# Wider up-projection matmuls, one-pass biased scores, summed head groups and later side work in a two-layer encoder kernel

## The chip, the cores and the metric

The kernel runs on 1 core of one Trainium2 chip. The metric is device time in microseconds (us): the median of 3 runs was 2298.27 us (2297.31 to 2302.01). Engines are named as in the profile: PE (TensorE matmuls), PEld (its weight loads), DVE (VectorE), ACT (ScalarE), POOL (GpSimd), SP (SyncE, whose queue issues the DMAs).

## What is computed

Two encoder layers on x of 256 tokens by 2048 features, all in fp32. The reference, cut to what matters:

```python
for layer in range(2):
    sh1, sc1, g1, sh2, sc2, g2 = split(silu(c) @ ada_w[layer] + ada_b[layer], 6)
    h = rms_norm(x, norm_g[layer, 0]) * (1 + sc1) + sh1
    y = local_dilated_mixer(h, ...) if layer == 0 else diff_attention(h, ...)
    x = x + g1 * rms_norm(y, norm_g[layer, 1])
    h = rms_norm(x, norm_g[layer, 2]) * (1 + sc2) + sh2
    gate, up = split(h @ w_up, 2)                       # 2 x 5504 columns
    gate = gate[t-1] * w[0] + gate[t] * w[1] + gate[t+1] * w[2] + b
    x = x + g2 * rms_norm((gelu(gate) * up) @ w_down, norm_g[layer, 3])
```

Layer 0's mixer has four heads A (one score map, window 128, a sink logit) and four heads B, each with three groups of queries over the same keys and values: the groups' softmax outputs are merged by their denominators, which is one softmax over the three score maps side by side. Layer 1's mixer has eight heads with two score maps each, whose softmaxes are subtracted (weight lambda). Every score has a bias of minus slope times distance.

## The kernel before

**The stream.** Every weight is read once, as tiles `raw` of 128x1024 fp32 (512 KB) in a ring of 9 buffers, in one fixed sequence of "units" (projection weights) and modulation tiles (`ada_w`). ACT rounds a unit to `whi` (fp32r, L248), DVE takes the rest `wlo = raw - whi` (L298); there are four buffers of this pair. A product of activation and weight is three matmuls: high by high, high by low, low by high. A modulation tile is not split: DVE multiplies it with a column of silu(c) and adds it to `aacc` (L273); after 16 tiles `ada_finish` sums over the partitions on PE (L433 and L441).

**Two forms of projection.** `tok_units` (L600 to L602) holds 128 tokens of activation as the stationary operand and streams 512 weight columns. `feat_units` (L629, L631, L632) holds 128x128 of a weight and streams 256 tokens, so a result has features on its partitions: per 128 rows of the contraction and 128 output features, `whi` by `hT` high, `whi` by `hT` low, `wlo` by `hT` high, three matmuls of 256 columns into the same half of a PSUM bank (`packed` holds two such halves). The FFN's gate and up projections and the queries and keys of both layers use it; the high and low parts of `hT` lie side by side, 2x256 columns.

**Order.** `st.done` after each unit is a tick: it starts the splits of the next units, runs the work that is due (`st.at`, `st.chain`, one stage of a chain per tick) and then emits the low parts. In layer 0's FFN and in the tails of the output stages the engines PE, DVE and ACT keep the program's order; elsewhere a scheduler places instructions. Layer 0's queries and keys are made in two halves of the contraction (`first_half` on ACT, `second_half` on DVE adds), then the heads run as chains among the units (`attn_a`, `attn_b`; in layer 1 `attn_c`).

**Around the change.** In `attn_b` DVE adds the bias to each of three maps (L737), takes the maximum over all (L740), ACT exponentiates with a sum (L745); two diagonal matrices with the reciprocal denominators (L477) normalise while PE transposes by matmul (`probs_T`, L672: three accumulating matmuls per 128x128 block). `attn_a` does the same with one map (L697, L698). In `attn_c` the bias and maximum are L780 and L782, the transposes L803. The convolution's weights come as rows (`crow`) that PE turns into columns (L387) 7 ticks after their load was issued.

## Time and profile before

| | before |
|---|---|
| median of 3 runs | 2298.27 us |
| the profiled execution: its own time | 2298.01 us |
| its span, first to last instruction | 2296.2 us |
| granted TensorE clock, mean share | 0.977 |
| PE busy | 2209.7 us (96%), 14953 matmul records |
| DVE busy | 1628.5 us (71%) |
| ACT busy | 1064.3 us (46%) |
| DMA | 588.18 MB, mean 256 GB/s |
| chain that ended last | PE 85%, issue 9%, DVE 2%, ACT 1%, DMA 1% |

In time order: modulation and layer 0's projections to about 190 us, its heads and output projection to 346, a tail of norms to 382, layer 0's FFN to 1120, layer 1's values from 1136, its heads from 1230 to 1475, its output projection to 1545, its FFN to 2278. A fp32 matmul (neither operand fp32r) leaves two records, so the 64 transposing matmuls of L672 are 128 records. The busy time of PE counts the modelled ends of pipelined matmuls; the pitch from start to start is what a matmul costs.

### The profile page before, as it was taken

To read this page: it belongs to the slowest core of one execution; us is meant where nothing else is said; L and a number is where in the kernel's file an instruction comes from. 1 tells how busy PE (TensorE), PEld (TensorE's weight loads), DVE (VectorE), ACT (ScalarE), POOL (GpSimd) and SP (SyncE) were. 2 spreads that over 40 slices of the span, in tenths; PEclk is the share of its full clock that TensorE was granted. 3 is DMA by queue.
4 is the path that set the end of the run, shared out by engine and by line. 5 is a ranking of instruction groups with operands and counts; after the bars stand their busy time and mean duration, and the time that the engine had idled before them with its cause. 6 is when DMAs were issued, how large, how long until landed. Compare 5 with 4: busy or idle time off the path is not lost.

```text
span 2296.2 us, 37376 instructions
## 1 busy us (share of the span) xinstructions
PE 2209.7 (96%) x14953; PEld 2029.4 (88%) x14953; DVE 1628.5 (71%) x1799; ACT 1064.3 (46%) x1463; POOL 42.4 (2%) x72
## 2 busy tenths in 40 slices
PE   4889989999999999999999999999999999999998
PEld 3888876999988999998779998879999888999986
DVE  7779997788776777876788996656656545565555
ACT  4433437454444444444644554456444444444443
POOL 0000000000000000000000100000000000000000
PEclk7989989999999999999999999999999999999999
DMA  9999998988889888997599996655667666667563
GB/s 363 343 329 321 303 340 274 308 287 289 286 287 303 290 285 288 294 294 252 170 337 329 305 306 206 217 179 176 206 198 203 200 203 207 196 202 203 178 186 104
DMA packets 390564, 588.18 MB, mean 256 GB/s; under 512 B 18123, under 2 KB 256373, under 8 KB 389621
## 3 DMA queue, kind: packets, MB, share of 16 engines
q1 hardware_dynamic: 390388, 585.79, 78.4%
q8 instruction: 117, 1.92, 0.4%
q14 instruction: 59, 0.48, 0.1%
HBM read 583.62 MB, written 2.10 MB: 255 GB/s over the span
## 4 chain that ended last, share of the span: by engine, by line
PE 85%; issue 9%; DVE 2%; ACT 1%; DMA 1%; POOL 0%; DVEq 0%; POOLq 0%; SPq 0%; ACTq 0%
PE bank L631 17%; PE bank L629 17%; PE bank L632 17%; PE bank L600 10%; PE bank L601 10%; PE bank L602 10%; DVE aacc L273 1%; PE bank L441 1%; PE bank L775 1%; ACT junk L473 1%; PE bank L812 0%; ACT whi L248 0%; DVE wlo L298 0%; PE bank L433 0%; PE bank L505 0%
## 5 line engine op out<-in xcount | busy, mean ns | idle before, releaser
L298 DVE TENSOR_TENSOR wlo<-raw,whi 128x1024 fp32r<-128x1024 f32 x708 | 860.7, 1219 | 492.6 <-ACT whi L248 473.7
L248 ACT ACTIVATE whi<-raw 128x1024 fp32r<-128x1024 f32 x708 | 745.5, 1055 | 963.6 <-PE bank L631 495.7
L629 PE MATMUL bank<-hT,whi 128*128 128x256 f32 x3616 | 1028.4, 285 | 0.0
L631 PE MATMUL bank<-hT,whi 128*128 128x256 f32 x3616 | 1020.1, 282 | 1.4 <-DVE hT L500 1.4
L632 PE MATMUL bank<-hT,wlo 128*128 128x256 f32 x3616 | 1019.6, 282 | 0.8 <-DVE wlo L298 0.8
L631 PEld LDWEIGHTS bank<-hT,whi 128*128 128x128 f32 x3616 | 687.4, 190 | 4.4 <-DVE hT L500 2.1
L629 PEld LDWEIGHTS bank<-hT,whi 128*128 128x128 f32 x3616 | 687.5, 190 | 2.7 <-ACT whi L248 1.0
L632 PEld LDWEIGHTS bank<-hT,wlo 128*128 128x128 f32 x3616 | 687.1, 190 | 1.4 <-DVE wlo L298 1.2
L273 DVE SCALAR_TENSOR_TENSOR aacc<-raw,ccol,aacc 128x1024 f32<-128x1024 f32 x352 | 455.2, 1293 | 49.8 <-DMA raw<-in_ada_w_dram 48.7
L600 PE MATMUL bank<-whi,act 128*128 128x512 f32 x656 | 259.3, 395 | 0.0
L601 PE MATMUL bank<-wlo,act 128*128 128x512 f32 x656 | 258.9, 395 | 0.0
L602 PE MATMUL bank<-whi,act 128*128 128x512 f32 x656 | 258.9, 395 | 0.0
L602 PEld LDWEIGHTS bank<-whi,act 128*128 128x128 f32 x656 | 123.4, 188 | 29.2
L600 PEld LDWEIGHTS bank<-whi,act 128*128 128x128 f32 x656 | 123.4, 188 | 29.0
L601 PEld LDWEIGHTS bank<-wlo,act 128*128 128x128 f32 x656 | 123.5, 188 | 28.9
L600 PE MATMUL bank<-whi,hT 128*128 128x512 f32 (+1 forms) x192 | 74.9, 393 | 8.5 <-ACT hT L496 8.5
L601 PE MATMUL bank<-wlo,hT 128*128 128x512 f32 (+1 forms) x192 | 74.6, 390 | 0.0
L600 PE MATMUL bank<-whi,oT 128*128 128x512 f32 x176 | 72.8, 414 | 1.0 <-DVE smb L737 1.0
L602 PE MATMUL bank<-whi,hT 128*128 128x512 f32 (+1 forms) x192 | 71.9, 384 | 0.0
L601 PE MATMUL bank<-wlo,oT 128*128 128x512 f32 x176 | 71.0, 404 | 0.0
L602 PE MATMUL bank<-whi,oT 128*128 128x512 f32 x176 | 70.6, 403 | 0.0
L441 PEld LDWEIGHTS bank<-ones,aacc 128*128 128x128 f32 x256 | 37.4, 227 | 25.2 <-issue 22.7
(171 smaller groups left out, 1363.8 us busy)
## 6 DMA issues: line engine op xcount, KB each, us to landing
raw<-in_ada_w_dram SPq DMA_DIRECT2D x384, 512.0 KB, 5.4
raw<-in_ffn_w_up_dram SPq DMA_DIRECT2D x344, 512.0 KB, 4.4
raw<-in_ffn_w_down_dram SPq DMA_DIRECT2D x168, 512.0 KB, 4.8
raw<-in_c_w_in_dram SPq DMA_DIRECT2D x96, 512.0 KB, 5.3
raw<-in_ab_w_in_dram SPq DMA_DIRECT2D x56, 512.0 KB, 5.9
raw<-in_c_w_out_dram SPq DMA_DIRECT2D x32, 512.0 KB, 5.2
raw<-in_ab_w_out_dram SPq DMA_DIRECT2D x16, 512.0 KB, 5.8
gb<-in_norm_g_dram SPq DMA_DIRECT2D x4, 1024.0 KB, 8.0
```

The costliest lines, as they stand in the source:

```text
L248: nc.scalar.activation(hi, v, AF.Copy)
L273: nc.vector.scalar_tensor_tensor(self.acc, t, col, self.acc, op0=ALU.mult, op1=ALU.add)
L298: nc.vector.tensor_tensor(lo, v, hi.bitcast(F32), op=ALU.subtract)
L441: nc.tensor.matmul(t[:, j:j + 1], acc[:, j * P:(j + 1) * P], ones[:, 0:1], start=True, stop=rows is None)
L473: nc.scalar.activation(j[:, :src.shape[1]], src, AF.Square, scale=n ** -0.5, accum_out=dst)
L600: nc.tensor.matmul(dst, ah, hi, start=first, stop=False, skip_group_check=True)
L601: nc.tensor.matmul(dst, ah, lo, start=False, stop=False, skip_group_check=True)
L602: nc.tensor.matmul(dst, al, hi, start=False, stop=last, skip_group_check=True)
L629: nc.tensor.matmul(acc[:, j], wh, hT[:, k, 0], start=k == begin and j == 0, stop=False, skip_group_check=True)
L631: nc.tensor.matmul(acc[:, j], wh, hT[:, k, 1], start=False, stop=False, skip_group_check=True)
L632: nc.tensor.matmul(acc[:, j], wl, hT[:, k, 0], start=False, stop=k == end - 1, skip_group_check=True)
L775: nc.tensor.matmul(s[t][:, j], q[:, j, t * P:(t + 1) * P], k[:, j], start=True, stop=True)
```

## The change

1. `feat_wide` takes the place of `feat_units` in the FFN's up-projections and in layer 1's queries and keys, except for the first seven blocks of layer 0's FFN and the first of layer 1's. `whi` meets high and low of `hT` in one matmul of 512 columns that fills a whole bank, `wlo` meets the high part with 256 columns added to its first half. A block of 256 features so takes two banks, and `both` puts the halves together: ACT copies the second half, DVE adds the first. In the FFN the sum lands in a new tile `gsum`, one tick after the block, from which convolution, taps and product read.
2. `biased` forms the biased scores and their maximum in one instruction (`tensor_tensor_reduce`); the query scale is divided by minus the slope so that (distance + score) times minus the slope is the biased score. It shows as an `ISA` row and a second one of 128x1 that reads the maximum out.
3. `attn_b` adds the three exponentiated maps of a head on DVE, ACT scales by the reciprocal, and `probs_T` is four plain transposes per head; `attn_a` scales likewise. The diagonals are gone.
4. The chain of `attn_c` starts one tick later; the convolution's rows are turned 11 ticks after their load instead of 7; `ada_finish` of the first gates (modulation 2) comes after 6 ticks instead of 2.

```diff
-                    self.at(2, lambda: ada_finish(l, ms, c0, w, acc, rows))
+                    self.at(6 if ms == (2,) else 2, lambda: ada_finish(l, ms, c0, w, acc, rows))
...
+    def feat_wide(n):
+
+        hT = cur["hT"]
+        accs = [packed() for _ in range(n // P)]
+        kt = 0
+        while kt < KT:
+            i, (hi, lo) = st.take()
+            a = hi.shape[1]
+            for b in range(a):
+                k = kt + b
+                for j, acc in enumerate(accs):
+                    nc.tensor.matmul(acc, hi[:, b, j * P:(j + 1) * P], hT[:, k], start=k == 0, stop=False,
+                                     skip_group_check=True)
+                    nc.tensor.matmul(acc[:, 0], lo[:, b, j * P:(j + 1) * P], hT[:, k, 0], start=False,
+                                     stop=k == KT - 1, skip_group_check=True)
+            kt += a
+            st.done(i)
+        return accs
...
+    def biased(dst, dist, s, slope, top):
+        nc.vector.tensor_tensor_reduce(dst, dist, s, -slope, LOWEST, ALU.add, ALU.max, top)
...
-        nc.scalar.activation(dst, acc, AF.Copy, scale=scale)
-
-    def second_half(dst, part, acc, scale=1.0):
-        nc.vector.scalar_tensor_tensor(dst, acc, scale, part, op0=ALU.mult, op1=ALU.add)
+        for d, a, m in scaled_by(scale, dst, acc):
+            nc.scalar.activation(d, a, AF.Copy, scale=m)
+    def second_half(dst, acc, scale=1.0):
+        for d, a, m in scaled_by(scale, dst, acc):
+            nc.vector.scalar_tensor_tensor(d, a, m, d, op0=ALU.mult, op1=ALU.add)
+    def scaled_by(scale, dst, acc):
+        if isinstance(scale, tuple):
+            return [(dst[:, i], acc[:, i], m) for i, m in enumerate(scale)]
+        return [(dst, acc, scale)]
+    def q_scale(*slopes):
+        return tuple(-QK_SCALE / m for m in slopes)
+    def kq_scale(g, hp):
+        if g == 0:
+            return (1.0, slope16(0) / slope16(1))
+        return q_scale(slope16(4 * g + 2 * hp))[0]
+    def both(dst, accs, scale=1.0):
+        for i, a in enumerate(accs):
+            nc.scalar.activation(dst[:, i], a[:, 1], AF.Copy, scale=scale)
+            nc.vector.scalar_tensor_tensor(dst[:, i], a[:, 0], scale, dst[:, i], op0=ALU.mult, op1=ALU.add)
+        return dst
+    def wide_pair(pool, scale, name):
+        accs = feat_wide(256)
+        return both(pool.tile([P, 2, S], F32, name=name, bufs=1), accs, scale)
...
-    def probs_T(pool, parts):
+    def probs_T(pool, e):
 
         pt = bank().rearrange("p (k q) -> p k q", k=2)
         for t in range(2):
             for kt in range(2):
-                for n, (e, d) in enumerate(parts[t]):
-                    nc.tensor.matmul(pt[:, kt, t * P:(t + 1) * P], e[:, kt * P:(kt + 1) * P], d,
-                                     start=n == 0, stop=n == len(parts[t]) - 1)
+                nc.tensor.transpose(pt[:, kt, t * P:(t + 1) * P], e[t][:, kt * P:(kt + 1) * P], ident)
...
-            nc.vector.scalar_tensor_tensor(sm, dist, -slope16(i), s, op0=ALU.mult, op1=ALU.add)
-            nc.vector.tensor_reduce(nm, sm, axis=AX.X, op=ALU.max)
+            for t in range(2):
+                biased(sm[:, t], dist[:, t], s[:, t], slope16(i), nm[:, t:t + 1])
...
+        def scale(r):
+            for t in range(2):
+                nc.scalar.activation(sm[:, t], sm[:, t], AF.Copy, scale=r[:, t:t + 1])
+
+        st.chain(scores, soft, expo, lambda _: scale(norm(None)),
+                 lambda _: probs_T(pool, [sm[:, t] for t in range(2)]),
...
+                top = small("top", 3)
                 for g in range(3):
-                    nc.vector.scalar_tensor_tensor(sm[:, g], dists[g][:, t], -slope16(4 + 4 * g + h), s[g],
-                                                   op0=ALU.mult, op1=ALU.add)
-                smf = sm.rearrange("p g k -> p (g k)")
-                nc.vector.tensor_reduce(nm[:, t:t + 1], smf, axis=AX.X, op=ALU.max, negate=True)
+                    biased(sm[:, g], dists[g][:, t], s[g], slope16(4 + 4 * g + h), top[:, g:g + 1])
+                nc.vector.tensor_reduce(nm[:, t:t + 1], top, axis=AX.X, op=ALU.max, negate=True)
...
+        def merge(t):
+            for g in range(1, 3):
+                nc.vector.tensor_add(sms[t][:, 0], sms[t][:, 0], sms[t][:, g])
+        def last(_):
+            expo(1)
+            merge(0)
         def norm(_):
             r = small("rden", 2)
             nc.vector.reciprocal(r, den)
+            merge(1)
             return r
-        def diags(r):
-            return [diag_of(r[:, t:t + 1]) for t in range(2)]
+        def scale(r):
+            for t in range(2):
+                nc.scalar.activation(sms[t][:, 0], sms[t][:, 0], AF.Copy, scale=r[:, t:t + 1])
...
-            for t in range(2):
-                nc.vector.scalar_tensor_tensor(sm[:, t], dd[:, t].unsqueeze(1).to_broadcast([P, 2, S]), -slope8(h),
-                                               s[t], op0=ALU.mult, op1=ALU.add)
-                nc.vector.tensor_reduce(nm[:, 2 * t:2 * t + 2], sm[:, t], axis=AX.X, op=ALU.max, negate=True)
+            for n in range(4):
+                t, j = n // 2, n % 2
+                biased(sm[:, t, j], dd[:, t], s[t][:, j], slope8(h), nm[:, n:n + 1])
+            nc.vector.tensor_scalar(nm, nm, -1.0, None, op0=ALU.mult)
...
-        st.chain(scores, soft, expo, norm, lambda _: None, turn, apply, rstd, scaled, back, finish)
+        st.chain(scores, soft, expo, norm, lambda _: None, turn, apply, rstd, scaled, back, finish, delay=1)
...
+            if isinstance(acc, list):
+                st.chain(lambda _: both(gsum(), acc), conv, taps, gelu)
+            else:
+                conv(acc)
+                st.chain(lambda _: taps(acc), gelu)
...
+            wide = isinstance(acc, list)
+            st.chain(*([lambda _: both(gsum(), acc)] if wide else []),
+                     lambda g: nc.vector.tensor_mul(c, (g if wide else acc)[:, :nj], c),
                      lambda _: nc.scalar.activation(ah, c, AF.Copy),
                      lambda _: nc.vector.tensor_tensor(act[:, j:j + nj, 1], c, ah.bitcast(F32), op=ALU.subtract))
...
-                            acc = packed()
-                            feat_units(acc, 0, KT, nj * P)
+                            acc = feat_wide(nj * P)
...
-                    st.at(7, lambda: to_columns(r, 2 * NF, cwc[l][:, half * 2 * NF:(half + 1) * 2 * NF]))
+                    st.at(11, lambda: to_columns(r, 2 * NF, cwc[l][:, half * 2 * NF:(half + 1) * 2 * NF]))
...
-            k = feat_pair(pool, 1.0, "kc")
-            q = feat_pair(pool, QK_SCALE, "qc")
+            k = wide_pair(pool, 1.0, "kc")
+            q = wide_pair(pool, -QK_SCALE / slope8(h), "qc")
```

Where instructions stand now. The first place is VectorE in layer 0, the first softmax of a head B (`smb` its scores, `dist1` to `dist3` the distances of the three groups, `nm` and `top` maxima, `aacc` modulation). Before:

```order
L737 SCALAR_TENSOR_TENSOR smb_1908<-dist1_120,bank_1867 128x256
L298 TENSOR_TENSOR wlo_1854<-raw_1709,whi_1853 128x1024
L273 SCALAR_TENSOR_TENSOR aacc_1506<-raw_1738,ccol_67,aacc_1506 128x1024
L737 SCALAR_TENSOR_TENSOR smb_1908<-dist2_123,bank_1867 128x256
L273 SCALAR_TENSOR_TENSOR aacc_1506<-raw_1742,ccol_67,aacc_1506 128x1024
L737 SCALAR_TENSOR_TENSOR smb_1908<-dist3_129,bank_1868 128x256
L656 SCALAR_TENSOR_TENSOR ka_269<-bank_1828,ka_269 128x512
L273 SCALAR_TENSOR_TENSOR aacc_1506<-raw_1775,ccol_67,aacc_1506 128x1024
L298 TENSOR_TENSOR wlo_1897<-raw_1771,whi_1896 128x1024
L273 SCALAR_TENSOR_TENSOR aacc_1506<-raw_1778,ccol_67,aacc_1506 128x1024
L740 TENSOR_REDUCE nm_1824<-smb_1908 128x1
```

Now:

```order
L657 ISA smb_1913,top_1914<-dist1_120,bank_1872 128x256
L657 ISA top_1914 128x1
L274 SCALAR_TENSOR_TENSOR aacc_1510<-raw_1746,ccol_67,aacc_1510 128x1024
L657 ISA smb_1913,top_1914<-dist2_123,bank_1872 128x256
L657 ISA smb_1913,top_1914<-dist3_129,bank_1873 128x256
L299 TENSOR_TENSOR wlo_1902<-raw_1775,whi_1901 128x1024
L274 SCALAR_TENSOR_TENSOR aacc_1510<-raw_1779,ccol_67,aacc_1510 128x1024
L785 TENSOR_REDUCE nm_1829<-top_1914 128x1
```

Each map is one pass with a readout behind it (the readout's row is shown once), and the last reduction goes over three numbers instead of 768.

The second place is layer 1's seventh head. `qc` is the query that its scores wait for, `on` the normalised output of the head before it, `rs_m` and `rs_r` the root mean square that `on` needs, `junk` the sums of squares it starts from. ScalarE before, and below it VectorE:

```order
L473 ACTIVATE junk_14065,css_14061<-bank_14056 128x256
L828 ACTIVATE on_14144<-bank_14056,rs_r_14098 128x256
L828 ACTIVATE on_14144<-bank_14056,rs_r_14102 128x256
L248 ACTIVATE whi_14091<-raw_13859 128x1024
L643 ACTIVATE qc_14105<-bank_13952 128x512
L248 ACTIVATE whi_14135<-raw_13900 128x1024
```

```order
L298 TENSOR_TENSOR wlo_14048<-raw_13817,whi_14047 128x1024
L273 SCALAR_TENSOR_TENSOR aacc_13659<-raw_14094,ccol_67,aacc_13659 128x1024
L466 TENSOR_REDUCE rs_m_14096<-css_14061 128x1
L466 TENSOR_REDUCE rs_m_14100<-css_14061 128x1
L298 TENSOR_TENSOR wlo_14092<-raw_13859,whi_14091 128x1024
```

Now, ScalarE and VectorE:

```order
L697 ACTIVATE qc_12756<-bank_12634 128x256
L249 ACTIVATE whi_12739<-raw_12552 128x1024
L697 ACTIVATE qc_12756<-bank_12635 128x256
L474 ACTIVATE junk_12751,css_12749<-bank_12744 128x256
L474 ACTIVATE junk_12753,css_12749<-bank_12744 128x256
L884 ACTIVATE on_12820<-bank_12744,rs_r_12793 128x256
L884 ACTIVATE on_12820<-bank_12744,rs_r_12797 128x256
L249 ACTIVATE whi_12782<-raw_12583 128x1024
```

```order
L698 SCALAR_TENSOR_TENSOR qc_12756<-bank_12634,qc_12756 128x256
L274 SCALAR_TENSOR_TENSOR aacc_12383<-raw_12742,ccol_67,aacc_12383 128x1024
L299 TENSOR_TENSOR wlo_12740<-raw_12552,whi_12739 128x1024
L698 SCALAR_TENSOR_TENSOR qc_12756<-bank_12635,qc_12756 128x256
L467 TENSOR_REDUCE rs_m_12791<-css_12749 128x1
L467 TENSOR_REDUCE rs_m_12795<-css_12749 128x1
```

On ScalarE the query now stands ahead of `on`, where it stood behind it; on VectorE the query's two sums stand on both sides of a modulation tile, with the root mean squares behind them.

## Rows read from the trace of the kernel before

**Rows 1.** The profile's page: busy time (share) and instructions, and the chain's shares.

```profile
PE 2209.7 (96%) x14953; PEld 2029.4 (88%) x14953; DVE 1628.5 (71%) x1799; ACT 1064.3 (46%) x1463; POOL 42.4 (2%) x72
PE 85%; issue 9%; DVE 2%; ACT 1%; DMA 1%; POOL 0%; DVEq 0%; POOLq 0%; SPq 0%; ACTq 0%
```

**Rows 2.** Busy time by stretch: PE, PEld, DVE, ACT, POOL (records), granted clock, DMA, GB/s.

```profile
190.00:240.00 50.00, 44.91 (x322) 42.01 (x321) 50.00 (x61) 17.33 (x23) 0.00 (x0) 0.97 1.00 356
240.00:290.00 50.00, 46.49 (x293) 41.68 (x292) 47.90 (x68) 23.23 (x51) 0.00 (x0) 0.97 0.89 299
290.00:334.00 44.00, 37.53 (x189) 30.86 (x187) 41.73 (x53) 20.26 (x37) 0.00 (x0) 0.93 0.96 338
800.00:1000.00 200.00, 200.00 (x1699) 200.00 (x1698) 157.33 (x166) 90.46 (x104) 0.00 (x0) 1.00 0.90 291
1230.00:1350.00 120.00, 119.81 (x959) 117.20 (x958) 108.17 (x127) 60.25 (x105) 10.10 (x10) 1.00 0.94 315
```

**Rows 3.** Stretches of one matmul form, PE alone: busy, records, granted clock, DMA, GB/s.

```profile
1600.00:1800.00 200.00, 200.00 (x1707) 1.00 0.69 201
1950.00:2050.00 100.00, 100.00 (x846) 1.00 0.69 197
690.00:750.00 60.00, 60.00 (x260) 1.00 0.90 303
1820.00:1900.00 80.00, 80.00 (x345) 1.00 0.64 201
```

**Rows 4.** Waits, all engines: who waited for whom, us in total, times, longest.

```profile
ACT whi L248 <- PE bank L631: 495.7, 318, 4.1
```

**Rows 5.** Timeline of DVE in layer 0's heads: start, us, engine, line, instruction.

```profile
195.17 1.27 DVE L273 SCALAR_TENSOR_TENSOR aacc<-raw,ccol,aacc 128x1024 f32<-128x1024 f32 x1
196.36 1.22 DVE L298 TENSOR_TENSOR wlo<-raw,whi 128x1024 fp32r<-128x1024 f32 x1
```

**Rows 6.** Groups by line and form: busy us, mean ns, idle before and its releaser.

```profile
L273 DVE SCALAR_TENSOR_TENSOR aacc<-raw,ccol,aacc 128x1024 f32<-128x1024 f32 x352 | 455.2, 1293 | 49.8 <-DMA raw<-in_ada_w_dram 48.7
L782 DVE TENSOR_REDUCE nm<-smc 128x2 f32<-128x512 f32 x16 | 10.6, 678 | 0.0
L780 DVE SCALAR_TENSOR_TENSOR smc<-dd,bank 128x512 f32<-128x512 f32 x16 | 10.6, 680 | 1.4 <-PE bank L775 1.4
L737 DVE SCALAR_TENSOR_TENSOR smb<-dist,bank 128x256 f32<-128x256 f32 x24 | 9.1, 409 | 0.0
L740 DVE TENSOR_REDUCE nm<-smb 128x1 f32<-128x768 f32 x8 | 7.5, 942 | 0.0
L661 DVE TENSOR_TENSOR oT<-bank,oT 128x256 fp32r<-128x256 f32 x8 | 3.3, 418 | 1.7 <-ACT oT L660 1.7
L466 DVE TENSOR_REDUCE rs_m<-css 128x1 f32<-128x2 f32 x16 | 1.9, 148 | 0.6 <-ACT junk L473 0.6
L787 ACT ACTIVATION_READ_ACCUMULATOR smc<-smc,nm 128x1 f32 x32 | 6.1, 191 | 0.0
```

**Rows 7.** Timeline of PE: transposes by matmul in layer 0.

```profile
244.97 2.84 PE L672 MATMUL bank<-diag,smb 128*128 128x128 f32 x24
```

**Rows 8.** Timeline at the end of layer 0's output projection: PE, then DVE.

```profile
333.63 0.41 PE L387 MATMUL bank<-ident,crow 86*128 86x86 f32 x1 [5.03 <-DMA crow<-in_ffn_conv_b_dram]
...
332.55 1.28 DVE L273 SCALAR_TENSOR_TENSOR aacc<-raw,ccol,aacc 128x1024 f32<-128x1024 f32 x1
```

**Rows 9.** Layer 1's heads: PE group of the scores, then timelines of DVE, ACT, PE.

```profile
L775 PE MATMUL bank<-kc,qc 128*128 128x256 f32 x64 | 16.9, 411 | 5.2 <-ACT qc L643 5.2
...
1419.32 1.28 DVE L273 SCALAR_TENSOR_TENSOR aacc<-raw,ccol,aacc 128x1024 f32<-128x1024 f32 x1 [3.86 <-DMA raw<-in_ada_w_dram]
...
1421.33 0.99 ACT L828 ACTIVATE on<-bank,rs_r 128x256 f32<-128x256 f32 x2 [5.36 <-POOL rs_r L468]
...
1423.80 3.50 PE L775 MATMUL bank<-kc,qc 128*128 128x256 f32 x8 [3.09 <-ACT qc L643]
```

More of the change, by code (lines that the diff above doesn't have):

```diff
@@ L22 @@
 BIG = 1e33
+LOWEST = -3e38
 HD = 128
@@ L710, in norm @@
             return r
-        def diags(r):
-            return [diag_of(r[:, t:t + 1]) for t in range(2)]
-        st.chain(scores, soft, expo, lambda _: diags(norm(None)),
-                 lambda d: probs_T(pool, [[(sm[:, t], d[t])] for t in range(2)]),
+        def scale(r):
[3 more added lines that the diff above has]
+                 lambda _: probs_T(pool, [sm[:, t] for t in range(2)]),
                  lambda pT: head_out(pool, oT, i, v, vc)(pT)(None), delay=delay)
@@ L749, in norm @@
             nc.vector.reciprocal(r, den)
+            merge(1)
             return r
-        def diags(r):
-            return [diag_of(r[:, t:t + 1]) for t in range(2)]
+        def scale(r):
+            for t in range(2):
+                nc.scalar.activation(sms[t][:, 0], sms[t][:, 0], AF.Copy, scale=r[:, t:t + 1])
         def mid(s):
@@ L761, in late @@
             soft(1)(s)
-        st.chain(scores(0), mid, late, lambda _: expo(1), norm, diags,
-                 lambda d: probs_T(pool, [[(sms[t][:, g], d[t]) for g in range(3)] for t in range(2)]),
+        st.chain(scores(0), mid, late, last, norm, scale,
+                 lambda _: probs_T(pool, [sms[t][:, 0] for t in range(2)]),
                  head_out(pool, oT, 4 + h, v, vc), lambda f: f(None), delay=delay)
@@ L1015, in ffn, with gsum, conv, taps @@
         cw = cwc[l]
+        def gsum():
+            return pool.tile([P, 2, S], F32, name="gsum", bufs=2)
         def gate(acc, cv, j, nj):
-            def taps(_):
+            def conv(g):
+                for i in range(nj):
+                    w = cw[:, NF + j + i:NF + j + i + 1]
+                    nc.scalar.activation(cv[:, i], g[:, i, :S], AF.Identity,
+                                         bias=cw[:, 3 * NF + j + i:3 * NF + j + i + 1], scale=w)
+                return g
+            def taps(g):
                 for i in range(nj):
@@ L1165, in encoder_kernel @@
         ka, qa0, qa1 = [pool.tile([P, 2, S], F32, name=n) for n in ("ka", "qa0", "qa1")]
-        late = [(ka, 1.0), (qa0, QK_SCALE), (qa1, QK_SCALE)]
-        late += [(d, QK_SCALE if g else 1.0) for g, d in enumerate(kq1)]
+        late = [(ka, 1.0), (qa0, q_scale(slope16(0), slope16(1))), (qa1, q_scale(slope16(2), slope16(3)))]
+        late += [(d, kq_scale(g, 1)) for g, d in enumerate(kq1)]
         def early_groups(half):
@@ L1183, in early_groups @@
             out = [(v[:, :, 0:256], va, 1.0)] + [(v[:, t, 256:768], v1[t], 1.0) for t in range(2)]
-            out += [(kq0[:, g], acc, QK_SCALE if g else 1.0) for g, acc in enumerate(kq)]
+            out += [(kq0[:, g], acc, kq_scale(g, 0)) for g, acc in enumerate(kq)]
             for d, acc, scale in out:
                 if half:
-                    second_half(d, d, acc, scale)
+                    second_half(d, acc, scale)
                 else:
@@ L1201, in rest @@
             feat_units(acc, 8, 8, 256, 8, KT)
-            second_half(d, d, acc, scale)
+            second_half(d, acc, scale)
         for l in range(2):
```

11 lines of the change are left out of this document (removed).

## The prediction

> **What bounds the kernel now.** I read the page's totals first, then busy time by stretch, then the groups of instructions, and the timeline where PE has a hole. The totals say that PE is 96% busy and makes 85% of the chain that ended last [rows 1]. The stretches say that this is an average over two regimes. In the FFNs PE never rests: in 800 to 1000 us it is busy for all 200 us, with DVE at 157 of 200 [rows 2]. From 190 to 334 us, layer 0's heads and output projection, it is the other way round: DVE is busy for 139.6 of 144 us (50.00, 47.90, 41.73) and PE for 128.9 [rows 2]. There a PE saving buys nothing and a DVE microsecond costs one. Layer 1's heads lie between: from 1230 to 1350 us PE is full and DVE at 108.2 of 120 [rows 2], and behind it PE has holes ahead of the scores, 5.2 us in all [rows 9].
>
> **1. The wide up-projection.** PE's price is the pitch of a form, taken from stretches that hold nothing else. 256 columns: 1707 records in 200 us, 846 in 100; less the three that an edge cuts, 117.4 and 118.6 ns, mean 118.0 [rows 3]. 512 columns: 260 in 60 us and 345 in 80; less two, 232.6 and 233.2, mean 232.9 [rows 3]. The clock is 1.00 in all four. Three matmuls of 256 cost 354.0 ns, one of 512 and one of 256 cost 350.9: 3.1 ns less, because a pitch is nearly proportional to its columns and the columns stay 768. How many: each layer's gate and up branch has 5504 columns, 43 blocks of 128 features, so 4 x 43 = 172, less 14 for the seven early blocks of 256 and 2 for layer 1's first: 156. Layer 1's heads have 8 x 2 x 2 = 32 (heads, query and key, halves). 188 x 16 contraction steps = 3008 triples, so **-9.3 us**, all in stretches where PE is full. The ends: nothing, if 512 costs two of 256 here (236.0); 34 us, if it costs one of 256 and 256 bare columns at 2.4 GHz (118.0 + 106.7 = 224.7). The value lies by the row of the same form.
>
> The Trainium skill, "TensorE: Matmul & The Clock Gate", section Back-to-back issue gap, gives N/2.4 + 2.5 ns per matmul: 109.2 and 215.8, so 2.5 ns per triple and 7.5 us. The rows are 8% above both of its figures and have the same small difference; by the page the sum would be 2 us smaller.
>
> **2. What pays for it.** `both` adds, per block of 128 features, an ACT copy and a DVE sum of 128x256. The nearest DVE row is L737 with one PSUM operand, 409 ns [rows 6]. Neighbours overlap by 0.08 us (195.17 + 1.27 against a next start at 196.36) [rows 5], so 0.33 us each: 1.3 us per FFN pair of 22.7 us (192 matmuls of 118 ns). DVE goes from 79% to 84% there. The cover holds: ACT's split sat idle 495.7 us until PE freed a buffer [rows 4], so the splits run ahead of PE and a sum or two delays nothing. Cost 0; without that cover it would be 156 x 0.33 = 51 us at most.
>
> **3. Layer 0's heads, where DVE sets the pace.** All prices less 0.08. Removed: 24 x 0.33 (L737), 8 x 0.86 (L740), 8 x 0.60 for L697 and L698 (the forms of L780 and L782), 4 x 0.60 for sums that are split by slope: 21.9 us [rows 6]. Added: 16 x 0.34 to sum groups (L661's form), 8 x 0.33 for the split sums, 8 x 0.07 for reductions over three numbers (L466): 8.6 us [rows 6]; and 32 fused passes with readout. No row shows these. Low end of a pass 0.33, as L737 of the same shape; high end 0.60, half of L780 plus half of L782 unfused. The readout is between 0.07 (L466) and 0.19 (ACT's own accumulator readout) [rows 6]. I take 0.33 + 0.13, nearest to a pass over the same operands: 14.7 us. Sum 23.3 against 21.9: +1.4. The ends: -0.5 (0.40 a pass) and +12 (0.79). Against this stands DVE's own idle time, 4.4 us of the 144 [rows 2], which is waiting for what PE has not done. PE becomes lighter here: 24 of the 128 records of L672 take 2.84 us, a pitch of 0.11, so 14.2 us go and 32 transposes of like size, 3.5, come [rows 7]. I credit half of the idle time, -2.2. Together **-1 us**; PE's 11 us as such stay hidden behind DVE.
>
> The later convolution rows are worth 0. The 5.03 us hole ahead of L387 looks like a price, but the matmuls that stand behind it need `aacc`, and DVE finishes that at 332.55 + 1.28 = 333.83, when they begin [rows 8]. If the row comes earlier or later, PE waits for DVE there. The later first gate moves two matmuls and two products of a gate and a load of 1 MB by four ticks, within the same full DVE: 0.
>
> **4. Layer 1's heads.** The holes have one history. A modulation tile stands ahead of the root mean square on DVE and waits 3.86 us for its DMA; so ACT's `on` waits 5.36; the query's copy stands behind `on`; PE waits 3.09 for it and then does eight records in 3.50 us [rows 9]. They took half that where the clock was full: 1.7 of loss. 5.2 + 1.7 = 7 us hang on that order. In the new order the copy is ahead of `on`, and the scores come a tick, one unit of 24 x 118 = 2.8 us, later. What is late next is the second sum of the query, behind a modulation tile: 1.2 + 1.1 + 2 x 0.33 after the block's end, 3 us against 5.6 of room, if the tile has landed. The DVE bill per head: 4 sums, 1.3, and fused passes 4 x 0.46 + 0.14 against 4 x 0.60: +0.9 us, times 4.4 heads in 1230 to 1350 us: 108 becomes 112 of about 118. That is tight, so I credit 5 of the 7: **-5 us** (ends -7 and +3).
>
> **Sum.** -9.3 - 1 - 5 = -15.3. The profiled execution took 2298.01 us by its own time (span 2296.2), 0.3 below the median, so 2283 for the median.
>
> **Rivals.** (a) *Wide buys nothing*: the 512 columns cost 236. For it: no row has this form with the weight stationary. Against: the column pitch of rows 3. It leaves parts 3 and 4, -6: 2292.
> (b) *The heads give nothing back*: DVE at 112 of 118 in layer 1 keeps some scores waiting, and layer 0 pays +3. For it: rows 2, 1230 to 1350 us. -9.3 + 3 = -6 to -10: 2290.
> (c) *Wide buys more*, toward 224.7 per 512 columns: -25 in part 1: 2267. Only the bare column count speaks for it.
> (d) *Slower*: the fused pass runs at half rate. 512 columns cost 0.27 more than 256 (680 against 409) [rows 6], so a pass would be 0.60 and 0.73 to 0.79 with its readout; layer 0 would pay 10 to 12 us and give back no idle time, and in layer 1 each head another 1.1 us, 117 to 119 of 118 in its first 120 us, which ends the gain there and costs some 5: -9.3 + 12 + 5 = +8: 2306. It decides from about 0.73 us per pass with readout. Against it: two fp32 SBUF operands do not halve L273, whose 1024 columns take 1293 ns, 1.2 ns per further column against 1.06 where one operand is PSUM [rows 6].
> The Trainium skill, "Vector Engine (DVE) Microarchitecture Reference", section Points that are easy to get wrong, says that this family of instructions halves its throughput with two SBUF sources that are not bf16, as no port is left for the accumulator. The pass here reads one SBUF and one PSUM source, and L273 contradicts the rule for a pass without accumulator; no row shows one with.
>
> **How the numbers follow.** Forecast 0.57; (a) 0.10; (b) 0.14; (c) 0.05; (d) 0.10; 0.04 for no change at all, if the scheduler lays the holes elsewhere and DVE eats the rest. Two thousandths, 4.6 us, is about what a measurement of this kernel can tell from no change. The forecast, (b), (c) and half of (a) are faster by more: 0.81. Half of (a) and the 0.04 are the same: 0.09. (d) is slower: 0.10. The range leaves out (d) and most of (c): from 2267 (part 1 at -17, the holes wholly gone, layer 0 at -5) to 2297.
>
> **What would show it.** In the FFNs of the changed profile a 512-column row by a 256-column one, together 351 ns, PE full and DVE near 84%; layer 0's heads still full on DVE, with a fused pass of about 0.41 and a readout under 0.2; no wait of the scores for `qc` in layer 1, or under 1 us. A triple at 354 or more, a pass of 0.6, or PE holes between 1230 and 1350 us would show steps 1, 3 or 4 wrong. If layer 0's stretch is shorter by PE's 11 us, DVE was not its bound, and my reading of rows 2 was.

## The result and the profile after

The changed kernel takes 2272.29 us (median of 4 runs, 2271.32 to 2273.63) against 2297.79 for the kernel before (2295.91 to 2302.01): a ratio of 0.9887, 95% interval 0.987 to 0.9904, or 25.5 us less. The forecast was 2283, 15 us less. The direction and the range held; the gain was larger than forecast, and it does not all lie where the forecast put it.

The page of the changed kernel, the rows that answer to [rows 1]:

```profile
PE 2176.4 (96%) x11849; PEld 1865.7 (82%) x11849; DVE 1682.5 (74%) x2079; ACT 1112.2 (49%) x1639; POOL 46.1 (2%) x72
PE 81%; issue 10%; DVE 4%; DMA 2%; ACT 2%; POOL 0%; DVEq 0%; POOLq 0%; SPq 0%; ACTq 0%
```

PE is as full as before with 3104 matmul records fewer. The stretches of [rows 2] (PE, PEld, DVE, ACT, POOL with records, granted clock, DMA, GB/s):

```profile
800.00:1000.00 200.00, 200.00 (x1162) 176.18 (x1161) 173.24 (x207) 103.62 (x142) 0.00 (x0) 1.00 0.91 297
190.00:240.00 50.00, 44.47 (x310) 41.21 (x309) 50.00 (x86) 19.98 (x30) 0.00 (x0) 0.97 0.97 340
240.00:290.00 50.00, 45.27 (x263) 39.17 (x262) 48.87 (x87) 23.46 (x49) 0.00 (x0) 0.97 0.97 343
290.00:334.00 44.00, 28.88 (x136) 22.72 (x134) 42.77 (x66) 18.33 (x33) 0.00 (x0) 0.87 0.93 323
1230.00:1350.00 120.00, 118.96 (x678) 103.69 (x677) 108.48 (x165) 61.97 (x116) 11.11 (x10) 1.00 0.92 311
```

In the FFN PE is still never idle, and DVE carries the sums at 173 of 200 us. The groups that are new, or answer to [rows 6] and [rows 9] (busy us, mean ns | idle before):

```profile
L644 PE MATMUL bank<-hT,whi 128*128 128x512 f32 x3008 | 1050.3, 393 | 0.0
L646 PE MATMUL bank<-hT,wlo 128*128 128x256 f32 x3008 | 840.9, 280 | 0.0
L657 DVE CUSTOM_DVE_ANT_0 smb<-dist,bank 128x256 f32<-128x256 f32 x32 | 12.6, 418 | 0.0
L657 DVE DVE_READ_ACCUMULATOR2_ANT top<- 128x1 f32 x24 | 2.1, 86 | 0.0
L698 DVE SCALAR_TENSOR_TENSOR gsum<-bank,gsum 128x256 f32<-128x256 f32 x156 | 62.1, 419 | 35.4 <-ACT gsum L697 35.4
L831 PE MATMUL bank<-kc,qc 128*128 128x256 f32 x64 | 15.1, 379 | 0.0
```

The fused pass (`CUSTOM_DVE_ANT_0`) takes 418 ns, its readout (`DVE_READ_ACCUMULATOR2_ANT`) 86, and the scores of layer 1 (L831) wait for nothing.

**Where the time went.** A stage is taken from the last PE matmul of one part to that of the next, by start times in the profiled executions (layer 0 to its tail's last L261 or L262, FFN by its last `hT,act`, values by `whi,hT`, output projection by `hT,oT`):

| us | before | after | difference |
|---|---|---|---|
| layer 0, heads, projection, tail | 370.06 | 368.10 | -1.96 |
| FFN 0 | 747.94 | 740.37 | -7.57 |
| values of layer 1 | 107.03 | 107.62 | +0.59 |
| heads of layer 1, projection | 312.82 | 304.87 | -7.95 |
| FFN 1 | 744.33 | 734.80 | -9.53 |

The two FFNs, where nothing but the up-projection and its sums has changed on PE, hold 17 of the 26 us; the forecast gave them 7.7 (2496 of the 3008 triples by 3.1 ns). Each column is one execution. Layer 0's -1.96 is no more than such executions differ by: with the old code of layer 0 it ended at 370.06 and, in run 1 below, at 368.70; with the new code, in this execution and four of the runs below (2, 3, 8 and 10), at 368.10 to 374.28.

**The pitch.** Two stretches of the FFN that hold only up-projections, for [rows 3] of before:

```profile
1600.00:1750.00 150.00, 150.00 (x867) 132.07 (x866) 101.82 (x126) 79.18 (x108) 0.00 (x0) 1.00 0.68 207
1950.00:2050.00 100.00, 100.00 (x579) 88.03 (x578) 67.22 (x83) 52.32 (x71) 0.00 (x0) 1.00 0.68 207
```

Less the three records that the edges cut, 432 pairs fill 150 us and 288 pairs 100: 347.2 ns in both, where 568 triples fill 200 us and 281 fill 100 [rows 3], 352.1 and 355.9. From start to start in the trace a 512-column matmul is followed after 229.2 ns and a 256-column one after 117.5, in both FFNs: 346.7 per pair. The forecast had 354.0 for the triple, which is right (the mean of a narrow matmul is 118.2 over FFN 0 and 117.9 over FFN 1), and 350.9 for the pair. 3008 x 7.3 = 22.0 us where it had 9.3.

### The profile page after: what moved, and what is told of

The parts are those of the page before. It is cut to its first block, busy times and chain, and to the rows that moved or that the text cites. A ratio compares the mean times of both kernels' runs of the same rounds, so it can differ in the third digit from the quotient of the medians.

```text
span 2269.5 us, 31605 instructions
## 1 busy us (share of the span) xinstructions
PE 2176.4 (96%) x11849; PEld 1865.7 (82%) x11849; DVE 1682.5 (74%) x2079; ACT 1112.2 (49%) x1639; POOL 46.1 (2%) x72
## 4 chain that ended last, share of the span: by engine, by line
PE 81%; issue 10%; DVE 4%; DMA 2%; ACT 2%; POOL 0%; DVEq 0%; POOLq 0%; SPq 0%; ACTq 0%
PE bank L644 29%; PE bank L646 15%; PE bank L596 9%; PE bank L598 9%; PE bank L597 9%; PE bank L627 2%; PE bank L625 2%; PE bank L628 2%; DVE aacc L274 2%; DMA raw<-in_ada_w_dram 1%; PE bank L442 1%; DVE wlo L299 1%; ACT junk L474 1%; PE bank L868 0%; ACT hf L487 0%
## 5 line engine op out<-in xcount | busy, mean ns | idle before, releaser
L299 DVE TENSOR_TENSOR wlo<-raw,whi 128x1024 fp32r<-128x1024 f32 x708 | 859.8, 1217 | 408.1 <-ACT whi L249 387.3
L644 PE MATMUL bank<-hT,whi 128*128 128x512 f32 x3008 | 1050.3, 393 | 0.0
L644 PEld LDWEIGHTS bank<-hT,whi 128*128 128x128 f32 x3008 | 564.7, 188 | 124.9 <-ACT whi L249 0.7
L274 DVE SCALAR_TENSOR_TENSOR aacc<-raw,ccol,aacc 128x1024 f32<-128x1024 f32 x352 | 454.2, 1290 | 28.1 <-DMA raw<-in_ada_w_dram 26.8
L625 PE MATMUL bank<-hT,whi 128*128 128x256 f32 x608 | 178.0, 293 | 0.0
L627 PE MATMUL bank<-hT,whi 128*128 128x256 f32 x608 | 175.5, 289 | 1.6 <-DVE hT L496 1.6
L627 PEld LDWEIGHTS bank<-hT,whi 128*128 128x128 f32 x608 | 119.4, 197 | 3.1 <-DVE hT L496 2.3
L625 PEld LDWEIGHTS bank<-hT,whi 128*128 128x128 f32 x608 | 119.4, 197 | 1.2 <-ACT hT L492 0.4
L698 DVE SCALAR_TENSOR_TENSOR gsum<-bank,gsum 128x256 f32<-128x256 f32 x156 | 62.1, 419 | 35.4 <-ACT gsum L697 35.4
L697 ACT ACTIVATE gsum<-bank 128x256 f32<-128x256 f32 x156 | 54.7, 373 | 59.8 <-PE bank L646 59.8
L596 PE MATMUL bank<-whi,hT 128*128 128x512 f32 (+1 forms) x192 | 75.1, 395 | 8.5 <-ACT hT L492 8.5
```

Of the source, the lines that this page charges most:

```text
L274: nc.vector.scalar_tensor_tensor(self.acc, t, col, self.acc, op0=ALU.mult, op1=ALU.add)
L299: nc.vector.tensor_tensor(lo, v, hi.bitcast(F32), op=ALU.subtract)
L596: nc.tensor.matmul(dst, ah, hi, start=first, stop=False, skip_group_check=True)
L625: nc.tensor.matmul(acc[:, j], wh, hT[:, k, 0], start=k == begin and j == 0, stop=False, skip_group_check=True)
L627: nc.tensor.matmul(acc[:, j], wh, hT[:, k, 1], start=False, stop=False, skip_group_check=True)
L644: nc.tensor.matmul(acc, hi[:, b, j * P:(j + 1) * P], hT[:, k], start=k == 0, stop=False, skip_group_check=True)
```

## The experiments

In all of them the ratio is to runs of the kernel before on the same chip. Where a run is compared with the changed kernel, that is its median, 2272.29.

**1 and 2. The wide form alone, and all but the wide form.** First the kernel before with only the FFN's wide matmuls and sums (`feat_wide`, `both` and `gsum` of the change), then the changed kernel with the three narrow ones:

```diff
-                            acc = packed()
-                            feat_units(acc, 0, KT, nj * P)
+                            acc = feat_wide(nj * P)
```

```diff
-                            acc = feat_wide(nj * P)
+                            acc = packed()
+                            feat_units(acc, 0, KT, nj * P)
...
-            k = wide_pair(pool, 1.0, "kc")
-            q = wide_pair(pool, -QK_SCALE / slope8(h), "qc")
+            k = feat_pair(pool, 1.0, "kc")
+            q = feat_pair(pool, -QK_SCALE / slope8(h), "qc")
```

> The kernel before with only the FFN's wide up-projection (156 blocks of 128 features, 2496 triples; conv, taps and product from the summed tile). Theory A (the pitch is shorter than forecast: the changed trace has 229.2 + 117.5 = 346.7 ns per pair against 354.0 for the three): 2496 x 7.3 = 18.2 us less, up to 2 given back by the sums: 2280 to 2282. Theory B (the forecast's 3.1 ns per triple holds, and the other 10 us come from the heads): 7.7 us less, 2290. If the sums were not covered by PE, less than 7 would be left.

> The changed kernel with the three 256-column matmuls back everywhere (no sums). Theory A: what is left is layer 0's 2 us and layer 1's holes, 4: 2291 to 2294. Theory B: the heads and the order carry 16 to 17 of the 25.5: about 2281. If the heads' part is worth nothing without the wide form: 2298.

The first took 2273.78 us (ratio 0.9896, 0.9882 to 0.9909), the second 2295.25 (0.9988, 0.9979 to 0.9996), before 2297.89. The wide FFN alone brings 24.1 us, and everything else without the wide form 2.6. Theory A is near in both, some 6 us too small in the first and 1 us outside in the second, and B falls; the wide form is worth 23.0 in the changed kernel (2295.25 - 2272.29). The first run brings 6 us more than the pitch gives (2496 x 7.3 = 18.2): its FFN stages are 19.9 shorter, and 3.4 come in the heads of layer 1, whose code it leaves alone, so their holes were laid elsewhere: PE waits 3.3 us for the query there, against 5.2 before. What moved them is not shown.

**3. The order of the same matmuls.** Both 512-column matmuls of a step first, then both of 256:

```diff
                 for j, acc in enumerate(accs):
                     nc.tensor.matmul(acc, hi[:, b, j * P:(j + 1) * P], hT[:, k], start=k == 0, stop=False,
                                      skip_group_check=True)
+                for j, acc in enumerate(accs):
                     nc.tensor.matmul(acc[:, 0], lo[:, b, j * P:(j + 1) * P], hT[:, k, 0], start=False,
```

> The changed kernel with the two 512-column matmuls of a step ahead of its two 256-column ones, instead of 512, 256, 512, 256. Theory P (price by form): the same, 2271 to 2273. Theory Q (alternation): half of the 3008 long ones at 233 instead of 229, 5 to 6 us more, 2278.

It took 2285.85 us (0.9943, 0.993 to 0.9956), 13.6 more than with 512 and 256 in turn. The same stretches as above:

```profile
1600.00:1750.00 150.00, 150.00 (x855) 130.51 (x854) 99.19 (x124) 77.08 (x106) 0.00 (x0) 1.00 0.69 203
1950.00:2050.00 100.00, 100.00 (x570) 86.99 (x569) 67.18 (x85) 52.49 (x73) 0.00 (x0) 1.00 0.69 202
```

426 pairs fill 150 us: 352.1 ns where the order in turn has 347.2. By start times the long one costs 233.7 here and the short one 118.0, together 351.7: the forecast's 350.9, nearly to the nanosecond. Neither theory had it right: not half of the long ones became dearer but all of them, and the short ones with them. 3008 x 5.0 = 15 us hang on the order of four matmuls alone. That order also changes which bank the neighbour of a matmul writes; no run here parts that from the order of lengths.

**4 and 5. The forms by themselves.** A kernel that only streams such matmuls, 256 units of each form (here the wide one):

```python
for k, j in W:
    mm(b2[j], wh(k, j), hT[:, k])
    mm(b2[j][:, 0], wl(k, j), hT[:, k, 0])
```

> No part of the reference's computation: matmuls of each form on their own, 256 pairs or triples of each, with nothing else running, then VectorE passes. Theory P (512 columns of activation against a stationary weight cost 229 ns whatever stands beside them): 229 in the section of such matmuls alone, 346.7 per pair in every order of the wide form; 352 to 356 per narrow triple; 233 for 512 columns of weight against stationary activation. Theory Q (what is cheap is the alternation of 512 and 256): 233 alone, 229 only beside 256. VectorE: a fused pass with one PSUM source 0.42 us, as in the changed trace; with two fp32 SBUF sources 0.42 if the source makes no difference, 0.60 to 0.70 if it halves the rate.

The stretches in turn: narrow, wide, 512 alone, 256 alone, 512 512 256 256, token form.

```profile
40.00:110.00 70.00, 70.00 (x585) 70.00 (x585) 0.00 (x0) 0.00 (x0) 0.00 (x0) 1.00 0.00 1
130.00:200.00 70.00, 70.00 (x398) 60.74 (x397) 0.00 (x0) 0.00 (x0) 0.00 (x0) 1.00 0.00 1
205.00:260.00 55.00, 55.00 (x245) 45.53 (x244) 0.00 (x0) 0.00 (x0) 0.00 (x0) 1.00 0.00 1
262.00:290.00 28.00, 28.00 (x235) 28.00 (x234) 0.00 (x0) 0.00 (x0) 0.00 (x0) 1.00 0.01 1
400.00:468.00 68.00, 68.00 (x392) 59.30 (x391) 0.00 (x0) 0.00 (x0) 0.00 (x0) 1.00 0.00 1
480.00:640.00 160.00, 160.00 (x707) 132.48 (x707) 0.00 (x0) 0.00 (x0) 0.00 (x0) 1.00 0.00 1
```

By start times: 120.0 per matmul of 256 alone and in the narrow triple (360), 226.7 per matmul of 512 alone and in the token form (680 per triple), but 353.3 per wide pair and 348.3 with the long ones first. Both theories fall: among its likes alone a matmul has one price (226.7 + 120.0 = 346.7 is the changed kernel's pair to the decimal), and elsewhere it can cost more or, as 117.4 in [rows 3], less. The order that is better in the kernel was the worse one here. So a second kernel put 40 units of each form behind five prefixes, twice, with loads and splits issued in the second half:

```python
for busy in range(2):
    for form, n in ((narrow, 7), (wide, 7), (tok, 13)):
        for prefix in (none, gap, small, four, half):
            prefix()
            form()
```

> No part of the reference's computation: sections of 40 narrow triples, wide pairs or token triples, each behind one of five prefixes (nothing, a wait for VectorE and one matmul of 512, one matmul of 128 columns, four of them, one of 256), first with nothing beside them, then with loads and splits on the DMA queue, ScalarE and VectorE. Theory R (the pitch is a rhythm that the start sets, and traffic does not): the same form comes out at different means behind different prefixes (226.7, 232.5 or 233.3 per 512 columns of the token form; 117.3, 118.7 or 120.0 narrow; 346.7 or 353.7 wide) and the second half repeats the first. Theory T (the traffic of the other engines sets it): the first half at 226.7 and 120.0 throughout, the second at 233 and 117 to 119.

Wide pairs straight behind the narrow section run at 353.3 ns (three pairs from 103.95 to 105.01):

```profile
103.95 0.40 PE L59 MATMUL bank<-hT,whi 128*128 128x512 f32 x1
...
105.01 0.40 PE L59 MATMUL bank<-hT,whi 128*128 128x512 f32 x1
```

and behind a wait and one matmul of 512 columns at 346.7 (three pairs from 117.80 to 118.84):

```profile
117.80 0.39 PE L59 MATMUL bank<-hT,whi 128*128 128x512 f32 x1
...
118.84 0.39 PE L59 MATMUL bank<-hT,whi 128*128 128x512 f32 x1
```

346.7 also came behind four matmuls of 128 columns and behind one of 256, 353.3 also behind one of 128. The second half, with DVE full, ACT at 90% and some 220 GB/s of loads, repeated all of it. The first half was not free of them, though: DVE and ACT ran ahead of PE in places, so the pairs behind the wait had company in both halves. Those straight behind the narrow section had none in the first half (the first line; the second is the pairs behind the wait):

```profile
98.00:107.00 9.00, 9.00 (x52) 7.81 (x52) 0.00 (x0) 0.00 (x0) 0.00 (x0) 1.00 0.00 0
111.00:121.00 10.00, 10.00 (x60) 8.81 (x59) 10.00 (x10) 9.01 (x10) 0.00 (x0) 1.00 0.68 204
```

Nor had those behind four matmuls of 128 and behind one of 256. On these three rests that, for the wide form, theory R holds: the start sets a rhythm (233, 117, 241, 120, 236, 113 ns over three pairs in one, 230 and 117 in another) that repeats to the end of the 40 pairs, and the traffic does not touch it. The token form came out at 680 per triple and the narrow at 360 behind every prefix at full clock, with such traffic too, so what gives them some 700 and 354 in the kernel is neither among the prefixes tried nor this traffic.

**6 and 7. The token form in another order**, first with its last two matmuls exchanged, then in turn between the token halves:

```diff
-        nc.tensor.matmul(dst, ah, lo, start=False, stop=False, skip_group_check=True)
-        nc.tensor.matmul(dst, al, hi, start=False, stop=last, skip_group_check=True)
+        nc.tensor.matmul(dst, al, hi, start=False, stop=False, skip_group_check=True)
+        nc.tensor.matmul(dst, ah, lo, start=False, stop=last, skip_group_check=True)
```

```diff
-                for t in range(2):
-                    mm_tok(dsts[t], act, ks[n + b], t, hi[:, b], lo[:, b],
...
+                for m in range(3):
+                    for t in range(2):
+                        nc.tensor.matmul(dsts[t], act[:, ks[n + b], m // 2, t * P:(t + 1) * P],
```

> The changed kernel with the three matmuls of the token form in the order high by high, low activation by high weight, high activation by low weight (the last two exchanged). Alone, a triple of this form took 680 ns; in the kernel it takes 700 (231 and 236 in turn). Theory R (the mean hangs on the order and on what goes ahead): the pitch of the down-projections moves from 233.3, anywhere between 226.7 (20 ns per triple, 1024 triples in the FFNs, outputs and values: 20 us less, 2252) and 236 (8 us more). Rival (233.3 is this form's price in this kernel whatever the order): 2272.

> The changed kernel with the token form's six matmuls of a step taken in turn between the two token halves (high by high for both, then the other two products likewise), so that neighbours write different banks. Theory R: again a pitch other than 233.3, with the time between 2252 and 2280. Rival: 2272.

2272.99 (0.9887, 0.9871 to 0.9904) and 2272.40 (0.9891, 0.9872 to 0.991): nothing. The pitch stayed at 231 and 236 in turn in FFN 0 and at 233 and 234 in FFN 1, a mean of 233.3 in both. The 6.7 ns between that and 226.7 alone stay unexplained.

**8. Sums twice.** Every sum of `both` a second time into a scratch tile:

```diff
             nc.vector.scalar_tensor_tensor(dst[:, i], a[:, 0], scale, dst[:, i], op0=ALU.mult, op1=ALU.add)
+            nc.vector.scalar_tensor_tensor(tmp.tile([P, S], F32, name="twice", bufs=1), a[:, 0], scale, dst[:, i],
+                                           op0=ALU.mult, op1=ALU.add)
```

> The changed kernel with every sum of `both` done a second time on VectorE into a scratch tile: 188 more passes of 0.42 us, 64 us of VectorE. Forecast (TensorE covers the sums in the FFNs; layer 1's heads are tight): 0 to 3 us more, 2272 to 2275. If the sums are not covered: up to 60 more.

2271.98 us (0.9888, 0.987 to 0.9906): no difference, with DVE at 186 of 200 us:

```profile
800.00:1000.00 200.00, 200.00 (x1161) 176.03 (x1160) 185.96 (x241) 103.67 (x143) 0.00 (x0) 1.00 0.90 297
```

**9. Fused passes twice.** `biased` issues its instruction twice.

```diff
         nc.vector.tensor_tensor_reduce(dst, dist, s, -slope, LOWEST, ALU.add, ALU.max, top)
+        nc.vector.tensor_tensor_reduce(dst, dist, s, -slope, LOWEST, ALU.add, ALU.max, top)
```

> The changed kernel with every fused pass of bias and maximum done twice (the same operands, the same result): 64 more passes of 0.418 us and 64 readouts on VectorE, less the overlap of neighbours 0.34 + 0.08 each, 13 us in layer 0's heads and 13 in layer 1's. Forecast (VectorE sets the pace in layer 0's heads, and layer 1's are tight): layer 0's part ends 10 to 13 us later, layer 1's heads 0 to 8; together 2283 to 2293. Rival (TensorE's holes and loads set the pace there, VectorE has room): within 3 us of 2272.

2278.75 us (0.991, 0.9893 to 0.9926), 6.5 more than the changed kernel, but not where the forecast's reading wants it: layer 0's stage ends at 368.12 us, with the changed kernel's 368.10. The work added there is some 11 us, not 13: the 32 extra passes start 0.34 us apart, readout included. Its DVE had even less idle time:

```profile
190.00:240.00 50.00, 42.79 (x286) 39.66 (x285) 50.00 (x105) 17.07 (x22) 0.00 (x0) 0.90 0.92 320
240.00:290.00 50.00, 42.27 (x253) 37.31 (x252) 48.40 (x89) 23.26 (x50) 0.00 (x0) 0.93 0.93 316
290.00:334.00 44.00, 36.52 (x155) 29.29 (x154) 44.00 (x98) 17.65 (x29) 0.00 (x0) 0.88 0.91 321
```

By 334 us four modulation tiles and two splits fewer were done than in the changed kernel (55, 2 and 28 records of L274, L270 and L299 against 58, 3 and 30): they slid behind 334 us, where the changed kernel's DVE stands idle for 7.17 us:

```profile
343.90 0.69 DVE L1063 TENSOR_TENSOR vy<-bank,gb 128x512 f32<-128x512 f32 x1 [7.17 <-ACT junk L474]
```

The heads themselves did become later. The last products of a head stand at 309.58 us in the changed kernel (first line) and at 325.68 with the passes twice (second line), 16.1 us later, where the five executions with the changed kernel's order there lie within 7 us; and PE's hole at the end of the stage, 12.79 us in the changed kernel (11 and 12 below), is down to 0.91 (third line):

```profile
309.58 1.05 PE L727 MATMUL bank<-pT,vy 128*128 128x256 f32 x4
325.68 1.09 PE L728 MATMUL bank<-pT,vy 128*128 128x256 f32 x4
329.08 0.29 PE L388 MATMUL bank<-ident,crow 86*128 86x86 f32 x1 [0.91 <-DVE oT L709]
```

So DVE's extra work did delay the heads, and the hole behind them swallowed the delay. FFN 0 became 3.2 us longer and layer 1's heads 4.1.

**10. No tick of delay in layer 1.**

```diff
-        st.chain(scores, soft, expo, norm, lambda _: None, turn, apply, rstd, scaled, back, finish, delay=1)
+        st.chain(scores, soft, expo, norm, lambda _: None, turn, apply, rstd, scaled, back, finish)
```

> The changed kernel with layer 1's heads started one tick earlier again (no delay of the chain). Theory F (the tick gives PE back the holes ahead of the scores, since both sums of the query stand between its block and the scores): 3 to 6 us more, 2275 to 2278. Rival (the order on ScalarE, query ahead of the normalised output, does it alone): within 1 us of 2272.

2283.05 us (0.9938, 0.9924 to 0.9951): 10.8 more than with the tick. In the profiled executions the heads' stage is 9.3 longer (314.12 against 304.87). PE's wait in layer 1's heads (us in total, times, longest):

```profile
PE bank L831 <- DVE qc L698: 8.2, 8, 1.6
```

Theory F has the mechanism, but its 3 to 6 us were too few: there are eight waits for the query's sum, as many as heads. That wait is the wide form's own; the narrow form has no sum, and there the scores waited for ACT's copy [rows 9].

**11 and 12. The hole at the end of layer 0.** First the rows of the convolution loaded earlier; then, in addition, eight column sums of the modulation behind 12 matmuls of the output projection (`soft` keeps them out of the flushes until then):

```diff
-                    st.at(11, lambda: to_columns(r, 2 * NF, cwc[l][:, half * 2 * NF:(half + 1) * 2 * NF]))
-                st.at(1 + 8 * (2 * l + half), load)
+                    st.at(7, lambda: to_columns(r, 2 * NF, cwc[l][:, half * 2 * NF:(half + 1) * 2 * NF]))
+                st.at(1 + 5 * (2 * l + half), load)
```

```diff
+                    soft = (l, ms, c0) == (0, (3, 4), 512)
-                    self.at(6 if ms == (2,) else 2, lambda: ada_finish(l, ms, c0, w, acc, rows))
+                    self.at(20 if soft else 6 if ms == (2,) else 2, lambda: ada_finish(l, ms, c0, w, acc, rows), soft=soft)
...
         for u in range(skew):
             run(0, u)
+        st.flush()
```

> The changed kernel with the four convolution rows loaded at ticks 1, 6, 11, 16 and turned 7 ticks later, so that no load is issued in the flush at the end of layer 0's heads, where PE now waits 12.8 us for one. Theory C (PE waits for that load, and behind it for the modulation tile that DVE finished 2 us earlier): 2 us less than the changed kernel, 2270. Theory D (the forecast's: DVE has the same work whenever the row comes, worth 0): 2272. Theory E (the whole hole is the row's): 8 us less, 2264.

> The changed kernel with the rows early as in the run before, and with the column sums of layer 0's third piece of the FFN's modulation moved behind the first two of the output projection's last four units on TensorE. With the rows early TensorE sat 9.7 us before these sums until VectorE had finished their tile. Theory G (the wait is one of order: work that is ready stands behind it): 12 matmuls, 2.8 us, move into the hole, so 2 to 3 us less than with the rows early alone, 2268 to 2269. Theory D (VectorE's work sets the end of layer 0 in any order): 2271 to 2272.

In the changed kernel the timeline of PE shows this hole, where [rows 8] has 5.03 us:

```profile
331.39 0.41 PE L388 MATMUL bank<-ident,crow 86*128 86x86 f32 x1 [12.79 <-DMA crow<-in_ffn_conv_b_dram]
331.59 3.48 PE L442 MATMUL bank<-ones,aacc 128*128 128x1 f32 x16
```

The load was issued at 324.70 us, and DVE had the tile for L442 ready by 329.33:

```profile
324.70 0.33 SPq L1278 DMA_DIRECT2D crow<-in_ffn_conv_b_dram  x1
```

```profile
326.73 2.60 DVE L274 SCALAR_TENSOR_TENSOR aacc<-raw,ccol,aacc 128x1024 f32<-128x1024 f32 x2
```

So PE did wait for the row, which came 2.1 us after the tile. With the rows early that wait is gone and another stands in its place, for the tile, which DVE finished later:

```profile
336.49 3.58 PE L442 MATMUL bank<-ones,aacc 128*128 128x1 f32 x16 [9.72 <-DVE aacc L274]
```

The times were 2271.42 (0.9886, 0.9873 to 0.99) and 2271.87 (0.9878, 0.9861 to 0.9894), the changed kernel's: theories E and G fall, and taking work or a load out of the hole brought nothing. The line of the rows early is from the slowest of their four executions (2275.49), which ended layer 0 at 373.25. None of the versions run beats the changed kernel by more than the runs scatter.

## Why the prediction was right, and where it was not

**Step 1, the wide form: the mechanism right, the size off by 2.4.** The term "350.9 for one of 512 and one of 256" failed: it measured 346.7, so -9.3 us was -22.0 by the pitch and -23.0 by the second run. It was taken from a 512-column row of stretches that hold that form alone [rows 3], on the assumption that a pitch belongs to a form. Its number was not wrong as such: with the long ones side by side the pair costs 351.7. In the kernel the order in turn is what pays, and no row before shows it. The upper end, 34 us by 342.7 per pair, held the value, and rival (c), 2267, was nearer in time than the forecast, though the long matmul cost 229.2 and not its bare 224.7. By the Trainium skill, "TensorE: Matmul & The Clock Gate", section Back-to-back issue gap, the term was 7.5 us; its figures for an isolated matmul, 109.2 and 215.8 ns, are below the 120.0 and 226.7 that each length took here among its likes alone.

**Step 2, the cover: right.** 156 sums at 419 ns cost nothing, nor do 188 more. DVE came to 87% in the FFN, not 84%.

**Step 3, layer 0: the sum near (-1 forecast, -2.0 in the profiled executions, which is within their scatter), its reason wrong.** "A DVE microsecond costs one" failed for layer 0's end: 11 us more on DVE did not move it. It delayed the heads, by 16 us in that execution, but not the stage: PE had a hole of 12.79 behind the heads to give, and DVE some load that could slide past 334 us, where it had room. The heads' pace was read as the stage's bound. The price of a fused pass was too high too: in the kernel of the forms passes with their readouts start 0.34 us apart, as if the readout were free, against 0.46 forecast, so 32 of them are 10.9 us and the ledger -2.4 instead of +1.4. That PE's 11 us stay hidden was right, but not that DVE hides them: the last product of a head starts 10.7 us earlier (310.25 against 320.97, L727 and L682), and the hole behind it grew from 5.03 [rows 8] to 12.79, so the tail begins at 348.61 instead of 350.56. That the later rows are worth 0 was right in the sum; that PE waits for DVE there and not for the row was so before, when row and tile came 0.2 us apart, and no longer in the changed kernel, where the row is the later by 2.1. What sets layer 0's end stays open. The run without the tick has the changed kernel's instruction order up to layer 1, and its profiled execution ended layer 0 at 374.28 instead of 368.10, with 293 against 311 GB/s loaded in 150 to 190 us; so the load stream is a candidate, not shown.

**Step 4, layer 1: the size near, the sense of it not.** The stage is 7.95 us shorter, 3.7 of that the wide form's 512 triples, which leaves 4.2 against the 5 forecast, and the scores wait for nothing. But the heads of run 1, with their old code, came out 3.4 shorter too, and those of run 2, with the new order and tick but no wide form, only 2.1, so the 4.2 cannot be put down to the order. And what the tick was shown to do is to keep new holes away: without it the wide form's own sums hold up the heads, eight times. Without the wide form the tick and the rest bring 2.6 us in the whole kernel, so of the -6 forecast for steps 3 and 4 less than half stands by itself. The forecast had too much for the heads and too little for the wide form, and the two partly cancelled. That the time lies in the range is partly luck: its lower end counts on no more than -17 from the wide form, which brought 22 to 23, and it held because the other parts, at -12 for that end, brought 2.6. The parts named for that end also add up to -29, which is 2269, not 2267.

**The rivals.** (a) fell: the wide form pays. (b) was as near for the heads by themselves (-2.6, between its 0 to +3 and the forecast's -6) and missed the wide form. (d) fell by the rows: a pass is 0.418, and in the kernel of the forms (4 above) two SBUF sources (first and third line) do not change it against one of PSUM (second and fourth), with an accumulator (first two) or without:

```profile
L131 DVE CUSTOM_DVE_ANT_0 e<-dist 128x256 f32<-128x256 f32 x16 | 5.6, 415 | 0.0
L127 DVE CUSTOM_DVE_ANT_0 e<-dist,bank 128x256 f32<-128x256 f32 x16 | 5.5, 415 | 0.0
L129 DVE SCALAR_TENSOR_TENSOR e<-dist 128x256 f32<-128x256 f32 x16 | 5.4, 416 | 0.0
L125 DVE SCALAR_TENSOR_TENSOR e<-dist,bank 128x256 f32<-128x256 f32 x16 | 5.4, 413 | 777.7 <-PE bank L58 777.7
```

The rule of the Trainium skill, "Vector Engine (DVE) Microarchitecture Reference", section Points that are easy to get wrong, by which two SBUF sources that are not bf16 halve the rate, is not borne out for these fp32 passes of 256 columns, with an accumulator or without.

## What to carry to other kernels

Price a matmul in the order in which it will stand: a row of the same length among its likes can be 2% off, and over thousands of matmuls in a full PE that was more than the rest of the change. An engine that is busy throughout a stage sets the stage's end only if all of its work there is due there and nothing behind it stands idle anyway; before a microsecond on it is priced at a microsecond, see what it carries for later and which hole follows. And a form that needs a sum behind it wants its consumer a step later, or the sum becomes the new wait.

## What the runs showed of the hardware that was not expected

- The pitch of fp32r matmuls is a rhythm with neighbours, at a clock of 1.00 throughout. Alone, 256 columns took 120.0 ns and 512 took 226.7. In the kernel before, 256 among its likes took 117.3 in some stretches of the FFNs and 118.7 in others; in the changed kernel it took 117.5 in turn with 512, which then took 229.2. In the kernels 512 took 232.4 to 233.7 among its likes. The same wide pairs on their own ran at 346.7 or 353.3 for 40 pairs, by what stood ahead of them, and a full DVE, a busy ACT and loads beside them changed nothing.
- The same order of instructions in layer 0 ended 6 us apart in two executions, with the load rate different ahead of it.
